# A decoder layer on one core: the causal mask of stick-breaking attention moves from TensorE to VectorE, and 1/rms per token comes back through DRAM

## The chip, the core and the metric

The kernel runs on one core of a Trainium2 chip. Five engines work side by side, each through its own instructions in order: TensorE (PE in the profile; its weight loads are PEld), VectorE (DVE), ScalarE (ACT), GpSimd (POOL) and SyncE (SP), which issues DMAs. Matrix products accumulate in PSUM, in banks of 128 partitions by 512 floats; everything else lies in SBUF, a 128-partition memory. Engines wait for each other on semaphores. The metric is the device time of one launch in microseconds (us).

## The reference, cut to what matters

One layer on 512 tokens of width 1024 (`D`): RMSNorm, one wide input projection, three attention branches (sliding window, stick-breaking, memory cross-attention), gates, an output projection, and a SwiGLU block. Two pieces matter here.

```
def rms_norm(x, g):
    y = xf * lax.rsqrt(jnp.mean(xf * xf, axis=-1, keepdims=True) + EPS)
    return y * g

def stick_breaking_attention(q, k, v):          # 8 heads of 64, blocks of 128 tokens
    z = einsum('bqhd,bkhd->bhqk', q_block, k[:, :L]) * d ** -0.5
    causal = arange(L)[None, :] < t
    log_1m = where(causal, log_sigmoid(-z), 0.0)
    between = cumsum(log_1m, axis=3, reverse=True) - log_1m
    a = where(causal, exp(log_sigmoid(z) + between), 0.0)
    out = einsum('bhqk,bkhd->bqhd', a, v)
```

## The kernel before, in words

Numbers are float32 throughout. A float32 matrix is cut into a high and a low part (`hi`, `lo`), and a product is three products of the fast 32-bit type (`mm3`, lines 164 to 168): ScalarE makes the high part (line 134), VectorE the low part (line 135). A plain float32 product, as in `mm` of line 171 with float32 operands, takes two passes on TensorE.

All weights pass through one stream, `dn`: a list of units, each of which has a load (SyncE), a split (ScalarE, VectorE) and a generator of products. The attention code of each head is a generator too; it gives up control with `yield us`, and `dn.run(us)` then emits so many microseconds of the stream's products by the kernel's own cost figures. These products are what TensorE has to do while the other engines work on the head. The framework's scheduler then fixes the order of every engine's instructions from priorities and its own estimates; on the chip each engine keeps to that order and waits where a semaphore is not there yet.

The normalization is applied late: projections run on x times the gain, and 1/rms multiplies their results. `rstd_of` (lines 218 to 234) takes per-position sums of squares `acc` (128 partitions; for the memory tokens two halves of 256 side by side). A product with an all-ones matrix adds over partitions and gives the sums on every partition, `ss`; four (two) products of one column give the same sums with a token per partition, `st`. Two reciprocal square roots follow: `rb`, token along the free axis, used where a projection is transposed; and `rs`, token on the partition, used where values are written (`v_all`, lines 333 to 339, and the memory values, line 398). The sum over the memory tokens, tile `mT`, is built by three GpSimd adds (line 368).

`sb_head` (lines 605 to 670) does one stick-breaking head. Keys lie on partitions, queries along the free axis, so the scores z are the upper part of a 4-by-4 grid of blocks: three PSUM banks hold 512, 384 and 256 + 128 columns (z of 0, 1 and 2; `SEG`). Eight score products fill them. Then four bf16 products of an identity with `negm` (-1e30 on and below the diagonal) are added onto the diagonal blocks: the mask (lines 626 and 627). For each bank ScalarE takes Abs, Exp and Ln, VectorE makes log(1 + e^z) from it (line 636, tile `e`), rounds it (`sh`, line 641) and takes the rest (`sl`, line 642). The head then yields 7.0 us. After that, products with triangular and all-ones matrices add the running sums onto the same three banks (lines 649 to 658, "the sums" below), ScalarE takes Exp, and two heads together are multiplied with the values into `ysb`, whose high part is `y10h` for the first pair.

PSUM has six banks for this work (`aps`), so two heads' scores fill them; the scores of head n+2 can only come when the banks of head n are free. Names with a number, as in the order below, are buffers of the program: a head's three banks are three numbers in a row. Projections that stand between the heads are `ka`, `qa`, `pmk` (memory keys), `pmv` and the gates `g`.

Of the kernel before, what the change touches and what calls it, by code (L numbers as in the profile page):

```python
# [10 lines left out]
F32 = mybir.dt.float32  # L11
F32R = mybir.dt.float32r
BF16 = mybir.dt.bfloat16
AF = mybir.ActivationFunctionType
ALU = mybir.AluOpType
AX = mybir.AxisListType

P = 128
D = 1024
S = 512  # L20
# [83 lines left out]
def tile_kernel(ctx, tc, a):  # L104
    nc = tc.nc
# [6 lines left out]
    drm = ctx.enter_context(tc.tile_pool(name="drm", bufs=1, space=bass.MemoryType.DRAM))  # L112
# [3 lines left out]
    cst = first.enter_context(tc.tile_pool(name="cst", bufs=1))  # L116

    def ck(name, dt=F32):
        return ckp.tile([P, 512], dt, tag="ck", name=name)

    def small(name, n=4):
        return sm.tile([P, 8], F32, tag="s", name=name)[:, :n]
# [4 lines left out]
    def aps(name):  # L127
        return psa.tile([P, 512], F32, tag="a", name=name)

    st = {}  # L130
# [33 lines left out]
    def mm3(out, l, r, start, stop):  # L164
        (lh, ll), (rh, rl) = l, r
        nc.tensor.matmul(out, lh, rh, start=start, stop=False, skip_group_check=True)  # L166
        nc.tensor.matmul(out, lh, rl, start=False, stop=False, skip_group_check=True)  # L167
        nc.tensor.matmul(out, ll, rh, start=False, stop=stop, skip_group_check=True)  # L168

    def mm(out, l, r, start, stop):  # L170
        nc.tensor.matmul(out, l, r, start=start, stop=stop, skip_group_check=True)  # L171

    def cols(hl, o, n):
        return hl[0][:, o : o + n], hl[1][:, o : o + n]
# [7 lines left out]
    def fn(*args, **kw):  # L182

        ins = nc.scalar.activation(*args, **kw)  # L184
        for p in pin:
            after(ins, p)
        since.append(ins)
        return ins
# [10 lines left out]
    def const(name, shape, pool=cst):  # L199
        t = pool.tile(shape, F32, name=f"c_{name}")  # L200
        nc.sync.dma_start(t[:, :], a[name])
        return t
# [3 lines left out]
    ones = cst.tile([P, P], F32, name="ones")  # L206
    nc.vector.memset(ones[:, :], 1.0)

    def rsqrt(r, v, t, ss):

        fn(t, ss, AF.Ln, bias=eps_t, scale=1.0 / D)
        nc.vector.tensor_scalar(v, ss, 1.0 / D, EPS, op0=ALU.mult, op1=ALU.add)
        fn(r, t, AF.Exp, scale=-0.5)
        nc.vector.scalar_tensor_tensor(t, r, -0.5, r, op0=ALU.mult, op1=ALU.mult)
        nc.vector.tensor_tensor(t, t, v, op=ALU.mult)
        nc.vector.scalar_tensor_tensor(r, t, 1.5, r, op0=ALU.add, op1=ALU.mult)

    def rstd_of(name, acc, n, bank):


        w = acc.shape[1] // n
        ps = bank(f"ss_{name}")
        for i in range(w):
            mm(ps[:, :n], ones[:, :], acc[:, i * n : (i + 1) * n], i == 0, i == w - 1)
        pt = bank(f"st_{name}")[:, : n // P] if n == S else ps[:, n : n + n // P]
        for t in range(n // P):
            for i in range(w):
                mm(pt[:, t : t + 1], acc[:, i * n + t * P : i * n + (t + 1) * P], ones[:, :1], i == 0, i == w - 1)
        rb = cst.tile([P, n], F32, name=f"rb_{name}")
        v, t = ck(f"v_{name}"), ck(f"t_{name}")  # L230
        rsqrt(rb[:, :], v[:, :n], t[:, :n], ps[:, :n])
        rs = cst.tile([P, n // P], F32, name=f"rs_{name}")
        rsqrt(rs[:, :], small(f"v_{name}", n // P), small(f"t_{name}", n // P), pt)
        return rs, rb

    def gained(x, g, h, l):
# [85 lines left out]
    def val(h, q):  # L322
        def gen(hi, lo):
            if q == 0:
                st["pv"] = [aps(f"pv{h}{t}") for t in range(NT)]
            for i in range(3 if q < 2 else 2):
                k = 3 * q + i
                for t in range(NT):
                    x = (u[k][0][:, t * P : (t + 1) * P], u[k][1][:, t * P : (t + 1) * P])
                    mm3(st["pv"][t][:, :320], x, cols((hi, lo), i * 320, 320), k == 0, k == KC - 1)  # L330
                    yield 0.41
                    if k == KC - 1:
                        nc.vector.tensor_scalar(
                            v_all[:, t * 640 + h * 320 : t * 640 + (h + 1) * 320],
                            st["pv"][t][:, :320],
                            st["rs"][:, t : t + 1],
                            None,
                            op0=ALU.mult,
                        )

        return gen

    v_all = cst.tile([P, NT * 640], F32, name="v_all")

    def vcols(t, lo):
        return v_all[:, t * 640 + lo : t * 640 + lo + 64]
# [87 lines left out]
    for h in range(2):  # L434
        for q in range(3):
            n = 3 if q < 2 else 2
# [111 lines left out]
    ident = const("ident", [P, P], base)  # L548
    ntri = const("ntri", [P, P])
    nmf = const("negm", [P, P])  # L550
    sinks = cst.tile([P, 8], F32, name="sinks")
    nc.sync.dma_start(sinks[:, :], a["sinks"].to_broadcast([P, 8]))
    identb = cst.tile([P, P], BF16, name="identb")
    nc.gpsimd.tensor_copy(identb[:, :], ident[:, :])
    negm = cst.tile([P, P], BF16, name="negmb")
    nc.gpsimd.tensor_copy(negm[:, :], nmf[:, :])
    ntri_r = cst.tile([P, P], F32R, name="ntri_r")
    nc.gpsimd.tensor_copy(ntri_r[:, :], ntri[:, :])
    none = cst.tile([P, P], F32, name="none")
# [38 lines left out]
    SEG = [(0, 0, 512), (1, 0, 384), (2, 0, 256), (2, 256, 128)]  # L598
    W = [512, 384, 384]

    def pair_out(b, c, ps):

        y[(b, c)] = parts(f"y{b}{c}", ps)

    def sb_head(h):
        c = h // 2
        ks, qs, ql = (st[(x, c, h % 2)] for x in ("kbs", "qbs", "qbl"))
        z = [aps(f"z{h}{i}") for i in range(3)]

        def seg(ts, j):  # L610
            i, o, n = SEG[j]
            return ts[i][:, o : o + n]

        for j in range(4):
            i, o, n = SEG[j]
            kj = slice(j * P, (j + 1) * P)
            if j < 3:
                out, qh, qlo = z[i][:, o : o + n], qs[:, j * P :], ql[:, j * P :]
            else:

                out = z[i][:, o : o + 2 * n]
                qh = qs[:, j * P :].unsqueeze(1).to_broadcast([P, 2, P])
                qlo = ql[:, j * P :].unsqueeze(1).to_broadcast([P, 2, P])
            mm(out, ks[:, kj], qh, j < 3, False)
            mm(out, ks[:, kj], qlo, False, False)
        for i, o, n in SEG:
            mm(z[i][:, o : o + P], identb[:, :], negm[:, :], False, False)
        e = [ck(f"e{h}{i}") for i in range(3)]
        sh = [ck(f"sh{h}{i}", F32R) for i in range(3)]
        sl = [ck(f"sl{h}{i}", F32R) for i in range(3)]  # L630
        for i in range(3):
            x, n = e[i][:, : W[i]], W[i]
            nc.scalar.activation(x, z[i][:, :n], AF.Abs)
            fn(x, x, AF.Exp, scale=-1.0)
            st["chain"] = fn(x, x, AF.Ln, bias=1.0)
            nc.vector.scalar_tensor_tensor(x, z[i][:, :n], 0.0, x, op0=ALU.max, op1=ALU.add)
            if i == 2:

                nc.vector.tensor_tensor(e[i][:, 384:], e[i][:, 128:256], e[i][:, 256:384], op=ALU.add)
                x, n = e[i][:, :], 512  # L640
            nc.vector.tensor_copy(sh[i][:, :n], x)
            nc.vector.tensor_tensor(sl[i][:, :n], x, sh[i][:, :n].bitcast(F32), op=ALU.subtract)
        yield 7.0

        def both(t):

            return t[2][:, :].rearrange("p (b n) -> p b n", b=4)[:, 0:4:3, :]

        for j in range(3):
            for t in (sh, sl):  # L650
                mm(seg(z, j), ntri_r[:, :], seg(t, j), False, j == 2 and t is sl)
        for t in (sh, sl):
            mm(z[0][:, 128:], none_r[:, :], seg(t, 1), False, False)
        for t in (sh, sl):
            mm(z[0][:, 256:], none_r[:, :], both(t), False, t is sl)
            mm(z[1][:, 128:384], none_r[:, :], both(t), False, t is sl)
        mm(z[2][:, 128:256], none[:, :], seg(e, 3), False, True)
        mm(seg(z, 3), ntri[:, :], seg(e, 3), False, True)
        for i in range(3):
            fn(e[i][:, : W[i]], z[i][:, : W[i]], AF.Exp)  # L660
        yield 3.0
        if h % 2 == 0:
            st["even"] = e
            return

        ys = aps(f"ysb{c}")
        for j in range(4):
            for i, x in enumerate((st["even"], e)):
                mm(ys[64 * i : 64 * i + 64, j * P :], vcols(j, 128 + (2 * c + i) * 64), seg(x, j), j == 0, j == 3)
        pair_out(SB, c, ys)  # L670
# [112 lines left out]
    for h in range(8):  # L783
        for us in sb_head(h):
            dn.run(us)
# [297 lines left out]
    rb = {}  # L1083
    bank = {}
# [316 lines left out]
```

## Time and profile before

| what | value |
|---|---|
| median of 3 runs | 818.17 us (818.04 to 818.42) |
| the profiled execution: its own time, and the span in the trace | 818.05 us, 816.3 us |
| TensorE busy | 806.5 us, 4753 products |
| VectorE busy | 590.2 us |
| ScalarE busy | 440.2 us |
| granted TensorE clock, mean | 0.999 |

A row of a timeline has the start in us from the span's beginning, the length in us, engine, line, operation, output and inputs, shapes, and how often it stands in a row (x). In brackets is how long the engine was idle before it and what ended that. An engine with Q behind its name (SPq) is the part that issues. A product's row on PE is longer than the time until the next one starts, since products overlap; what one costs in a row of others is the distance between two starts. The eight heads fill the stretch from 81 us to 215 us.

### The profile page before, as it was taken

How to read it: one execution, taken by the hardware profiler on the slowest of the kernel's cores; microseconds unless marked ns; L12 is line 12 of the kernel's file. 1: busy time of each engine (PE TensorE's matmuls, PEld its weight loads, DVE VectorE, ACT ScalarE, POOL GpSimd, SP SyncE). 2: the span in 40 equal slices, each digit the busy share in tenths (PEclk: the TensorE clock that was granted, in tenths of full speed). 3: DMA queues.
4: the chain of work that ended last, by engine and by line, in shares of the span. 5: the costliest groups of instructions: out<-in, count | busy, mean ns of one | idle time of the engine just before them, and what ended most of it. 6: DMA issues, size and time to landing. Idle time of an engine off the chain costs nothing.

```text
span 816.3 us, 12397 instructions
## 1 busy us (share of the span) xinstructions
PE 806.5 (99%) x4753; PEld 706.6 (87%) x4753; DVE 590.2 (72%) x945; ACT 440.2 (54%) x791; POOL 82.7 (10%) x100
## 2 busy tenths in 40 slices
PE   9999999999999999999999999999999999999996
PEld 6899888778788888888888899999999999988885
DVE  7796768556488853774385869977776767798797
ACT  7453757556555542553362666644444455666573
POOL 3002200000000000231003200010000000205200
PEclk9999999999999999999999999999999999999999
DMA  7434524321221223212359945977777763759902
GB/s 267 141 114 128 190 87 128 85 73 52 78 78 53 78 78 102 79 53 78 103 155 352 254 93 142 247 199 201 183 189 178 185 178 94 169 131 223 213 1 103
DMA packets 37563, 112.93 MB, mean 138 GB/s; under 512 B 4352, under 2 KB 6064, under 8 KB 37504
## 3 DMA queue, kind: packets, MB, share of 16 engines
q1 hardware_dynamic: 29184, 86.32, 33.5%
q0 software_dynamic: 7888, 25.43, 16.4%
q8 instruction: 37, 0.61, 0.3%
q10 hardware_dynamic: 432, 0.39, 0.1%
q14 instruction: 22, 0.18, 0.1%
HBM read 108.46 MB, written 3.67 MB: 137 GB/s over the span
## 4 chain that ended last, share of the span: by engine, by line
PE 94%; DVE 3%; ACT 1%; DMA 1%; issue 0%; ACTq 0%; SPq 0%; DVEq 0%
PE g L166 5%; PE g L167 5%; PE g L168 5%; PE gx L166 5%; PE gx L168 5%; PE gx L167 5%; PE z L171 4%; PE br L166 3%; PE br L167 3%; PE br L168 3%; PE gy L168 3%; PE gy L166 3%; PE gy L167 3%; PE x L167 2%; PE x L166 2%; PE x L168 2%
## 5 line engine op out<-in xcount | busy, mean ns | idle before, releaser
L134 ACT CAST hi<-raw 128x1024 fp32r<-128x1024 f32 (+2 forms) x64 | 65.8, 1034 | 110.1 <-issue 50.2
L134 ACT CAST hi<-gw 128x1024 fp32r<-128x1024 f32 x77 | 79.8, 1048 | 82.2 <-DVE gw L986 40.0
L135 DVE TENSOR_TENSOR lo<-gw,hi 128x1024 fp32r<-128x1024 f32 x77 | 93.5, 1223 | 33.6 <-ACT hi L134 33.6
L135 DVE TENSOR_TENSOR lo<-raw,hi 128x1024 fp32r<-128x1024 f32 (+2 forms) x64 | 78.1, 1220 | 17.6 <-ACT hi L134 17.3
L166 PE MATMUL g<-uh,hi 128*128 128x512 f32 x192 | 75.6, 394 | 0.0
L168 PE MATMUL g<-uh,lo 128*128 128x512 f32 x192 | 74.8, 389 | 0.0
L167 PE MATMUL g<-ul,hi 128*128 128x512 f32 x192 | 74.8, 389 | 0.0
L288 DVE SCALAR_TENSOR_TENSOR g<-g,rb_x 128x512 f32<-128x512 f32 x24 | 16.4, 690 | 55.4 <-PE g L168 55.3
L168 PEld LDWEIGHTS g<-uh,lo 128*128 128x128 f32 x192 | 36.0, 188 | 7.6
L166 PEld LDWEIGHTS g<-uh,hi 128*128 128x128 f32 x192 | 36.1, 188 | 7.5 <-issue 0.3
L968 POOL DMA_DIRECT2D gw<-in_w_gu x27 | 23.4, 905 | 188.8 <-DMA gw<-in_w_gu 81.4
L167 PEld LDWEIGHTS g<-ul,hi 128*128 128x128 f32 x192 | 36.1, 188 | 7.1
L134 ACT CAST hi<-r 128x1024 fp32r<-128x1024 f32 (+1 forms) x24 | 23.6, 982 | 19.9 <-PE y L168 5.3
L167 PE MATMUL x<-lo,lh 128*128 128x512 f32 x88 | 34.2, 389 | 0.0
L166 PE MATMUL x<-hi,lh 128*128 128x512 f32 x88 | 34.2, 389 | 0.0
L168 PE MATMUL x<-hi,ll 128*128 128x512 f32 x88 | 34.1, 389 | 0.0
L135 DVE TENSOR_TENSOR lo<-r,hi 128x1024 fp32r<-128x1024 f32 (+1 forms) x24 | 27.1, 1131 | 3.7 <-ACT hi L134 3.6
L184 ACT ACTIVATE e<-e 128x384 f32<-128x384 f32 (+1 forms) x48 | 26.9, 561 | 1.5
L134 ACT CAST hi<-bp 128x512 fp32r<-128x512 f32 x33 | 19.1, 619 | 13.4 <-PE y L168 4.8
L135 DVE TENSOR_TENSOR lo<-bp,hi 128x512 fp32r<-128x512 f32 x33 | 22.3, 711 | 5.0 <-ACT hi L134 4.9
L166 PE MATMUL gx<-T4h,hi 128*128 128x256 f32 x88 | 25.1, 285 | 0.4 <-ACT hi L134 0.4
L166 PE MATMUL gy<-N22h,hi 128*128 128x256 f32 x88 | 25.1, 285 | 0.2 <-ACT hi L134 0.2
(546 smaller groups left out, 2618.1 us busy)
## 6 DMA issues: line engine op xcount, KB each, us to landing
gw<-in_w_gu SPq DMA_DIRECT2D x57, 512.0 KB, 5.1
raw<-in_w_p SPq DMA_DIRECT2D x38, 512.0 KB, 3.6
gw<-in_w_gu POOLq DMA_DIRECT2D x27, 512.0 KB, 7.9
raw<-in_w_br SPq DMA_DIRECT2D x12, 512.0 KB, 3.8
bp<-in_w_dn SPq DMA_DIRECT2D x22, 256.0 KB, 8.4
r<-in_w_dn POOLq DMA_DIRECT2D x10, 512.0 KB, 8.7
raw<-in_w_out SPq DMA_DIRECT2D x8, 512.0 KB, 3.6
bp<-in_w_dn POOLq DMA_DIRECT2D x11, 256.0 KB, 12.8
```

The costliest lines, as they stand in the source:

```text
L134: ins = nc.scalar.copy(hi, raw)
L135: lows = nc.vector.tensor_tensor(lo, raw, hi.bitcast(F32), op=ALU.subtract)
L166: nc.tensor.matmul(out, lh, rh, start=start, stop=False, skip_group_check=True)
L167: nc.tensor.matmul(out, lh, rl, start=False, stop=False, skip_group_check=True)
L168: nc.tensor.matmul(out, ll, rh, start=False, stop=stop, skip_group_check=True)
L171: nc.tensor.matmul(out, l, r, start=start, stop=stop, skip_group_check=True)
L184: ins = nc.scalar.activation(*args, **kw)
L288: nc.vector.scalar_tensor_tensor(t[:, :], ps[:, :], s, st["rb"][:, :], op0=ALU.mult, op1=ALU.mult)
L968: nc.gpsimd.dma_start(gw[(n, key)][:, :], g_src(n, i, j), accum_op=ALU.add)
```

## The change: mask on VectorE, 1/rms per token by DMA

Three things change. First, the four mask products of each head go, and with them the bf16 copies of the identity and of `negm` that GpSimd made; instead VectorE adds the float32 `negm` onto the diagonal block of each bank in PSUM, one instruction for each of the first two banks (128 columns) and one for the two blocks of the third (2 x 128). The head's first yield is 8.5 instead of 7.0. Second, the one-column products and the second reciprocal square root go; the first row of `rb` is written to DRAM and read back with a token per partition, by two DMAs of GpSimd, the second waiting for the first. For the memory tokens the two halves of the sums of squares are now added by VectorE, so that one product of ones is left of two. Third, the evictions into `v_all` are emitted at high priority.

```
     def rstd_of(name, acc, n, bank):
-        w = acc.shape[1] // n
+        if acc.shape[1] > n:
+            nc.vector.tensor_tensor(acc[:, :n], acc[:, :n], acc[:, n : 2 * n], op=ALU.add)
         ps = bank(f"ss_{name}")
-        for i in range(w):
-            mm(ps[:, :n], ones[:, :], acc[:, i * n : (i + 1) * n], i == 0, i == w - 1)
-        pt = bank(f"st_{name}")[:, : n // P] if n == S else ps[:, n : n + n // P]
-        for t in range(n // P):
-            for i in range(w):
-                mm(pt[:, t : t + 1], acc[:, i * n + t * P : i * n + (t + 1) * P], ones[:, :1], i == 0, i == w - 1)
+        mm(ps[:, :n], ones[:, :], acc[:, :n], True, True)
         rb = cst.tile([P, n], F32, name=f"rb_{name}")
         v, t = ck(f"v_{name}"), ck(f"t_{name}")
         rsqrt(rb[:, :], v[:, :n], t[:, :n], ps[:, :n])
+        row = drm.tile([1, n], F32, name=f"row_{name}")
+        nc.gpsimd.dma_start(row[:, :], rb[:1, :])
         rs = cst.tile([P, n // P], F32, name=f"rs_{name}")
-        rsqrt(rs[:, :], small(f"v_{name}", n // P), small(f"t_{name}", n // P), pt)
+        nc.gpsimd.dma_start(rs[:, :], row[:, :].rearrange("o (t p) -> (o p) t", p=P))
         return rs, rb
...
                     if k == KC - 1:
-                        nc.vector.tensor_scalar(
+                        with tc.high_priority():
+                            nc.vector.tensor_scalar(
...
     def sb_head(h):
...
-        for i, o, n in SEG:
-            mm(z[i][:, o : o + P], identb[:, :], negm[:, :], False, False)
+        for i in range(3):
+            x, m = z[i][:, :P], nmf[:, :]
+            if i == 2:
+                x, m = z[i][:, :].rearrange("p (b n) -> p b n", b=4)[:, 0:4:2, :], m.unsqueeze(1).to_broadcast([P, 2, P])
+            nc.vector.tensor_tensor(x, x, m, op=ALU.add)
...
-        yield 7.0
+        yield 8.5
```

The order of the built program moves with it. Lines of the changed file are a few lower than those before.

**First place: VectorE at the first two heads.** Before, after the last instruction that belongs to the bias (`brow`), VectorE goes straight to head 0, whose banks are z_887, z_888 and z_889:

```order
L582 TENSOR_TENSOR brow<-pbias,wm 128x384
L636 SCALAR_TENSOR_TENSOR e_902<-z_887,e_902 128x512
L641 CAST sh_905<-e_902 128x512
L642 TENSOR_TENSOR sl_908<-e_902,sh_905 128x512
L636 SCALAR_TENSOR_TENSOR e_903<-z_888,e_903 128x384
L641 CAST sh_906<-e_903 128x384
L642 TENSOR_TENSOR sl_909<-e_903,sh_906 128x384
```

In the changed program the banks of head 0 are z_873 to z_875 and those of head 1 z_1045 to z_1047:

```order
L578 TENSOR_TENSOR brow<-pbias,wm 128x384
L627 TENSOR_TENSOR z_873<-z_873,c_negm 128x128
L627 TENSOR_TENSOR z_874<-z_874,c_negm 128x128
L627 TENSOR_TENSOR z_875<-z_875,c_negm 128x2x128
L627 TENSOR_TENSOR z_1045<-z_1045,c_negm 128x128
L627 TENSOR_TENSOR z_1046<-z_1046,c_negm 128x128
L627 TENSOR_TENSOR z_1047<-z_1047,c_negm 128x2x128
L636 SCALAR_TENSOR_TENSOR e_887<-z_873,e_887 128x512
L641 CAST sh_890<-e_887 128x512
L642 TENSOR_TENSOR sl_893<-e_887,sh_890 128x512
L636 SCALAR_TENSOR_TENSOR e_888<-z_874,e_888 128x384
L641 CAST sh_891<-e_888 128x384
```

The masks of head 0 come first, as written. Then the three masks of head 1 stand ahead of everything that VectorE does for head 0 after its mask (`e_887` and on). On TensorE the scores of head 1 come behind the 24 products of `ka`, and directly behind them the sums of head 0. This is TensorE in the changed program from the last score product of head 1 on:

```order
L171 MATMUL z_1047<-qbl_428,kbs_305 128x256
L171 MATMUL z_1047<-qbs_427,kbs_305 128x256
L171 MATMUL z_1047<-qbl_428,kbs_305 128x256
L171 MATMUL z_873<-sh_890,ntri_r 128x512
L171 MATMUL z_873<-sl_893,ntri_r 128x512
L171 MATMUL z_874<-sh_891,ntri_r 128x384
L171 MATMUL z_873<-sh_891,none_r 128x384
L171 MATMUL z_874<-sl_894,ntri_r 128x384
L171 MATMUL z_873<-sl_894,none_r 128x384
L171 MATMUL z_875<-sh_892,ntri_r 128x256
L171 MATMUL z_873<-sh_892,none_r 128x256
L171 MATMUL z_874<-sh_892,none_r 128x256
```

Between the scores of head 1 and the sums of head 0 nothing else stands, neither before nor now; before, the four masks stood there.

**Second place: TensorE at heads 2 and 3.** Before, the products with the values of the first pair (`ysb`) were followed by all eight scores of head 2 and its masks, and 54 products of `pmk` later by the sums of head 2. In the changed program the four score products of head 2's first two banks went ahead, and the third bank's scores follow the values:

```order
L171 MATMUL ysb_1228<-e_1061,v_all 64x128
L171 MATMUL z_1243<-qbs_466,kbs_309 128x256
L171 MATMUL z_1243<-qbl_467,kbs_309 128x256
L171 MATMUL z_1243<-qbs_466,kbs_309 128x256
L171 MATMUL z_1243<-qbl_467,kbs_309 128x256
L166 MATMUL pmk_1206<-mh_811,hi_1034 128x256
L167 MATMUL pmk_1206<-ml_812,hi_1034 128x256
```

From here 27 products of `pmk` with 256 columns follow, the first two of which end the rows above; then the scores of head 3 (z_1408 to z_1410) and the sums of head 2 (z_1241 to z_1243) alternate:

```order
L171 MATMUL z_1408<-qbs_472,kbs_312 128x512
L171 MATMUL z_1408<-qbl_473,kbs_312 128x512
L171 MATMUL z_1241<-sh_1258,ntri_r 128x512
L171 MATMUL z_1409<-qbs_472,kbs_312 128x384
L171 MATMUL z_1409<-qbl_473,kbs_312 128x384
L171 MATMUL z_1241<-sl_1261,ntri_r 128x512
L171 MATMUL z_1410<-qbs_472,kbs_312 128x256
L171 MATMUL z_1410<-qbl_473,kbs_312 128x256
L171 MATMUL z_1410<-qbs_472,kbs_312 128x256
L171 MATMUL z_1410<-qbl_473,kbs_312 128x256
L171 MATMUL z_1242<-sh_1259,ntri_r 128x384
L171 MATMUL z_1241<-sh_1259,none_r 128x384
```

Eight more products on the second and the third bank follow, the last three of them with `sl_1263`, and one with an `e` ends the sums. On VectorE the three masks of head 3 stand inside head 2's work: one of z_1408 and one of z_1409 ahead of `e_1256`, one of z_1410 ahead of `sh_1259`. What moved: `pmk` products that stood between the values and head 2's sums now stand ahead of the values.

**Third place: VectorE at heads 4 and 5.** Before, the third bank of head 4:

```order
L636 SCALAR_TENSOR_TENSOR e_1567<-z_1552,e_1567 128x384
L639 TENSOR_TENSOR e_1567<-e_1567 128x128
L641 CAST sh_1570<-e_1567 128x512
L135 TENSOR_TENSOR lo_1610<-raw_1495,hi_1609 128x1024
L642 TENSOR_TENSOR sl_1573<-e_1567,sh_1570 128x512
```

In the changed program the first mask of head 5 (z_1711) stands in the middle of it:

```order
L636 SCALAR_TENSOR_TENSOR e_1581<-z_1567,e_1581 128x384
L639 TENSOR_TENSOR e_1581<-e_1581 128x128
L627 TENSOR_TENSOR z_1711<-z_1711,c_negm 128x128
L641 CAST sh_1584<-e_1581 128x512
L135 TENSOR_TENSOR lo_1621<-raw_1507,hi_1620 128x1024
L642 TENSOR_TENSOR sl_1587<-e_1581,sh_1584 128x512
```

On TensorE the eight scores of head 5 stand, now as before, among the sums of head 4, ahead of the products with head 4's last `sl`.

More of the change, by code (lines that the diff above doesn't have):

```diff
@@ L332, in gen @@
                     if k == KC - 1:
[L333 to L339, printed above, removed]
+                        with tc.high_priority():
+                            nc.vector.tensor_scalar(
+                                v_all[:, t * 640 + h * 320 : t * 640 + (h + 1) * 320],
+                                st["pv"][t][:, :320],
+                                st["rs"][:, t : t + 1],
+                                None,
+                                op0=ALU.mult,
+                            )
         return gen
@@ L552, in tile_kernel @@
     nc.sync.dma_start(sinks[:, :], a["sinks"].to_broadcast([P, 8]))
[L553 to L556, printed above, removed]
     ntri_r = cst.tile([P, P], F32R, name="ntri_r")
```

## The prediction

> **What bounds the kernel now.** I read the page's busy times first, then the chain that ended last, then windows over the stretches in which the heads run.
>
> ```profile
> PE 806.5 (99%) x4753; PEld 706.6 (87%) x4753; DVE 590.2 (72%) x945; ACT 440.2 (54%) x791; POOL 82.7 (10%) x100
> PE 94%; DVE 3%; ACT 1%; DMA 1%; issue 0%; ACTq 0%; SPq 0%; DVEq 0%
> 80.00:88.50 8.50, 8.50 (x48) 6.89 (x47) 5.19 (x12) 5.09 (x10) 1.07 (x1) 1.00 0.71 246
> 88.50:95.00 6.50, 6.38 (x39) 5.48 (x38) 4.50 (x11) 3.40 (x7) 3.92 (x6) 1.00 0.53 155
> 114.00:128.00 14.00, 14.00 (x106) 12.60 (x105) 9.46 (x16) 8.67 (x14) 0.00 (x0) 1.00 0.21 53
> 157.00:163.00 6.00, 6.00 (x39) 5.43 (x38) 5.14 (x8) 2.50 (x4) 0.00 (x0) 1.00 0.40 99
> ```
>
> In a window the figures after its length are the busy times of PE, PEld, DVE, ACT and POOL, then the granted clock. TensorE sets the time: it is busy in 806.5 of 816.3 us and in nearly all of the four stretches. So a product that goes is time gained, and any wait that TensorE has not now is time lost. VectorE has idle time (72% busy), but it works in order, and what it makes TensorE wait for is the question of this case.
>
> **What is removed.** The mask of head 0, the one-column products of x, and both sums of the memory tokens, on TensorE:
>
> ```profile
> 82.96 0.40 PE L171 MATMUL z<-negmb,identb 128*128 128x128 bf16 x4
> 83.16 0.48 PE L166 MATMUL ka<-uh,hi 128*128 128x512 f32 x1
> 83.48 0.40 PE L167 MATMUL ka<-ul,hi 128*128 128x512 f32 x1
> 83.71 0.40 PE L168 MATMUL ka<-uh,lo 128*128 128x512 f32 x1
> 23.73 0.95 PE L171 MATMUL st_x<-ones,xacc 128*128 128x1 f32 x8
> 24.54 0.48 PE L166 MATMUL kb<-uh,hi 128*128 128x512 f32 x1
> 85.33 1.02 PE L171 MATMUL ss_m<-mT,ones 128*128 128x256 f32 x4
> 86.20 0.95 PE L171 MATMUL ss_m<-ones,mT 128*128 128x1 f32 x8
> 87.01 0.48 PE L166 MATMUL ka<-uh,hi 128*128 128x512 f32 x1
> ```
>
> The four mask products go from 82.96 to 83.16: 0.20 us. The product behind them needs 0.32 us to its successor (83.16 to 83.48), where the next needs 0.23 (83.48 to 83.71); those 0.09 us I count to the mask too. So 0.29 a head, 2.3 us for eight; 1.6 if the change of type costs the same elsewhere. The one-column products of x take 24.54 - 23.73 = 0.81. Of the memory tokens' sums half of 86.20 - 85.33 goes, 0.43, and the one-column products, 87.01 - 86.20 = 0.81. **Removed: 2.3 + 0.81 + 1.24 = 4.4 us**, at least 3.7.
>
> **What the masks cost on VectorE.** No row of before has VectorE writing PSUM, so the price is bounded by rows of the same operation or with one operand in PSUM:
>
> ```profile
> 81.67 0.56 DVE L582 TENSOR_TENSOR brow<-pbias,wm 128x384 f32<-128x384 f32 x1 [0.22 <-PE pbias L171]
> 85.18 0.69 DVE L636 SCALAR_TENSOR_TENSOR e<-z,e 128x512 f32<-128x512 f32 x1 [2.96 <-ACT e L184]
> 85.91 0.43 DVE L641 CAST sh<-e 128x512 fp32r<-128x512 f32 x1
> 88.43 0.55 DVE L636 SCALAR_TENSOR_TENSOR e<-z,e 128x384 f32<-128x384 f32 x1
> 89.02 0.29 DVE L639 TENSOR_TENSOR e<-e 128x128 f32<-128x128 f32 x1
> 89.76 1.22 DVE L135 TENSOR_TENSOR lo<-raw,hi 128x1024 fp32r<-128x1024 f32 x1
> 90.89 0.69 DVE L642 TENSOR_TENSOR sl<-e,sh 128x512 fp32r<-128x512 f32 x1
> ```
>
> 512 columns with z take 0.69 and 384 take 0.55, so 128 columns are 0.14 and the fixed part about 0.13: 0.27 for 128 columns, 0.41 for two blocks of 128. The 128-column row of line 639 (0.29) agrees. Bounds: 0.15 (the slope alone) and 0.69 (the longest row with z) for each. A head's three masks are 0.95, eight heads 7.6 us of VectorE; alone these lie beside TensorE. What matters is where they stand.
>
> **First stall: heads 0 and 1.** By the order shown ahead, head 1's masks stand in VectorE's queue before the first instruction that head 0 needs from it (`e_887`). They need head 1's scores. On TensorE these come after the 24 products of `ka`, and directly behind them come head 0's sums, which need `sh` and `sl`. So the chain of VectorE for head 0, which ran beside `ka` from 85.18 to 91.58 (90.89 + 0.69), now begins only when head 1's last score has landed, and TensorE has nothing else in its queue.
>
> ```profile
> 91.66 0.28 PE L171 MATMUL z<-qbl,kbs 128*128 128x256 f32 x1
> 91.78 0.40 PE L171 MATMUL z<-negmb,identb 128*128 128x128 bf16 x4
> 91.99 0.48 PE L171 MATMUL z<-sh,ntri_r 128*128 128x512 f32 x1
> 93.58 0.28 PE L171 MATMUL z<-sl,ntri_r 128*128 128x256 f32 x1
> ```
>
> From the issue of the last score (the row at 91.66) to the third bank's `sl`: the score's own length 0.28, the third mask 0.41 (the first two end earlier), the chain 91.58 - 85.18 = 6.40, a handover 0.05: 7.14 us. In that time TensorE does the score's own 0.12 (91.66 to 91.78) and the sums that do not need the last `sl`, 1.5 (91.99 to 93.58 is 1.59; a little of it comes late). **Stall 7.14 - 1.62 = 5.5 us.** With masks at 0.15 it is 5.2, at 0.69 5.8; if the `lo` of 1.22, which stands in the chain in both programs, finds another place, 4.4.
>
> **Second stall: heads 2 and 3.** Now 54 products of `pmk` stand between head 2's masks and its sums; in the changed program 27, and the third bank's scores come only behind the values. ScalarE, in order, makes `y10h` before it starts on head 2:
>
> ```profile
> 116.52 0.59 ACT L134 CAST y10h<-ysb 128x512 fp32r<-128x512 f32 x1 [3.18 <-PE ysb L171]
> 118.08 0.60 ACT L633 ACTIVATE e<-z 128x512 f32<-128x512 f32 x1 [0.98 <-PE z L171]
> 125.69 0.68 DVE L642 TENSOR_TENSOR sl<-e,sh 128x512 fp32r<-128x512 f32 x1
> ```
>
> From `y10h` to the last `sl` of head 2 it is 126.37 - 116.52 = 9.85; the idle 0.98 for z disappears, since its first banks stand ready, so 8.87. Head 3's three masks stand inside this chain, 0.95, and the wait between queues another 0.15: 9.95. TensorE's work from the last value product to the products with that last `sl`, at the distances of before (0.12 for 256 columns, 0.17 for 384, 0.23 for 512): the four scores 0.5, 27 `pmk` products 3.2, head 3's scores (0.46 + 0.35 + 0.46 = 1.3), and those sums of head 2 that stand ahead, some 1.5. Together 6.5. **Stall 9.95 - 6.5 = 3.4 us**; without the masks' share 2.5, with masks at 0.69 4.5.
>
> **Third stall: heads 4 and 5.** The first mask of head 5 stands before the rounding of head 4's third bank (`sh_1584`), and waits for head 5's first scores, which TensorE emits in the middle of head 4's sums.
>
> ```profile
> 157.71 0.43 DVE L641 CAST sh<-e 128x512 fp32r<-128x512 f32 x1
> 159.19 0.69 DVE L642 TENSOR_TENSOR sl<-e,sh 128x512 fp32r<-128x512 f32 x1
> ```
>
> From that score's issue: 0.23 to the second of the two, its length 0.39, mask 0.27, then `sh` to the end of `sl`, 159.88 - 157.71 = 2.17, handover 0.1: 3.16. TensorE has 1.64 of head 5's remaining scores and head 4's sums to do meanwhile. **Stall 1.5 us** (1.4 to 2.0 with the mask's bounds). Between head 6's last score and its sums the changed order has 39 products of 512 columns, 9.0 us at 0.23; the chain there, as at head 2 from ScalarE's first row for z, is 126.37 - 118.08 = 8.3, and the sums with the last `sl` come later still. So nothing there, and the same for head 7.
>
> Strict order within VectorE's queue carries all three. [...] No single row of before decides it outright.
>
> **What I cost at nothing.** The round trip of 1/rms: `rb_x` is ready at 28.5, and the first reader of `rs_x` is `v_all` at 66.7.
>
> ```profile
> 27.79 0.69 DVE L216 SCALAR_TENSOR_TENSOR rb_x<-t_x,rb_x 128x512 f32<-128x512 f32 x1
> bscr<-brow POOLq DMA_DIRECT2D x1, 1536.0 KB, 6.5
> bias<-bscr POOLq DMA_DIRECT2D x4, 256.0 KB, 6.0
> 15.69 4.45 POOL L268 MEMSET qbl<- 64x512 f32 x8
> 66.71 1.92 DVE L333 TENSOR_SCALAR v_all<-pv,rs_x 128x320 f32<-128x320 f32 x4
> 66.86 1.28 POOL L368 TENSOR_TENSOR mT<-mT,mT 128x512 f32<-128x512 f32 x1 [1.09 <-ACT mT L364]
> 67.30 0.42 PE L166 MATMUL pv<-hi,uh 128*128 128x320 f32 x1 [0.33 <-DVE v_all L333]
> ```
>
> The nearest DMAs of GpSimd (a write to DRAM, 6.5 us, and reads of it, 6.0) make 13 us: landed at about 42, cover 25 us. The eight memsets of `qbl`, 4.45 us, stand behind the two DMAs on GpSimd now; they would end before 50, and head 0 needs them at 81. If the cover were gone, `v_all` and with it TensorE would wait for the rest.
>
> The halves of the memory sum are a case of their own: VectorE adds them ahead of a `lo` and of `v_all`, and must wait for GpSimd's third add, which ends at 68.14 (66.86 + 1.28). If that stays, the first `v_all` ends at 68.14 + 0.42 + 0.81 + 0.48 and TensorE goes on at 69.9 instead of 67.30: +2.6. GpSimd's adds start when the memory tiles have come, and these loads stand behind a weight load whose buffer is freed by a VectorE instruction that the new order puts some 2 us earlier, TensorE being 0.8 ahead as well. I take 0; bounds -0.3 (the wait of 0.33 that `v_all` causes now) and +2.6.
>
> **The sum.** -4.4 + 5.5 + 3.4 + 1.5 = +6.0. On the profiled execution's 818.05 (span 816.3, and 1.75 around it, which the change leaves) that is 824.05; the median is 0.1 above the profiled execution. Forecast **824.0**. Its own bounds: -4.4 + 4.4 + 2.5 + 1.4 = +3.9 and -3.7 + 5.8 + 4.5 + 2.0 = +8.6, so 821.9 to 826.7.
>
> **The rivals.**
> - *Only the first pair stalls* (0.10). The first stall has nothing in TensorE's queue to cover it; the other two are differences of two estimated sums of 10 and 3 us. If the masks are half as long and the stream's products suffice there: -4.4 + 5.5 = +1.1, 819.2. Against it: half of `pmk` has left the place.
> - *The memory sum holds `v_all` up* (0.10): 6.0 + 2.6 = +8.6, 826.6. For it the rows at 66.71 and 66.86: GpSimd's add ends after `v_all` starts. Against it the earlier loads.
> - *The other side: the order does not hold TensorE up* (0.05). VectorE takes a mask when its scores are there and does head 0's work before; then only the removal stays, -4.4, 813.7. It decides if less than 4.4 of stalls is left. For it: VectorE has 28% idle. Against it: each row of VectorE in the first chain starts where the one before ends, in the order written.
> - *The clock falls in the gaps* (0.06).
>
> ```profile
> 810.00:814.00 4.00, 0.00 (x0) 0.00 (x0) 2.55 (x6) 0.71 (x4) 0.00 (x0) 1.00 0.50 187
> 814.00:816.30 2.30, 0.00 (x0) 0.00 (x0) 0.00 (x0) 0.00 (x0) 0.00 (x0) 0.60 0.25 93
> ```
>
> At the end TensorE does nothing from 810 on; the clock is 1.00 for four more us and 0.60 after them. The forecast's longest single gap is about 2 us (mask, `e`, `sh` of the first bank), with sums in between, so I expect 1.00. If half speed came for 4 us of one stall, 2 us more: 826 for one, 830 for all three. [...]
> - *`rs_x` late* (0.03): if the round trip took 50 us instead of 13, `v_all` would wait until 78, up to 11 us more, 835.
>
> **How the numbers follow.** Forecast 0.66, rivals 0.10, 0.10, 0.05, 0.06, 0.03. No change means within 0.2%, 1.6 us, which is what a measurement of this kernel can tell. Slower by more: forecast, memory sum, clock and late `rs_x`, 0.85, less 0.01 for the forecast's lower end, 0.84; within: the first-pair case, 0.09, and that 0.01, 0.10; faster: 0.05 and 0.01 of the first-pair case with less stall, 0.06. The range takes in the first-pair case below and the memory sum above: **819.0 to 827.0**; out stay the faster side, the clock, late `rs_x` and a little of each edge.
>
> **What would show it.** Right: VectorE idle for about 6 us between head 0's masks and its first `e`, ended by TensorE's scores of head 1; TensorE with some 5.5, 3.4 and 1.5 us of idle, ended by VectorE, at the three places; the masks' rows at 0.27 and 0.41; `v_all` started by products, not by GpSimd; the two small DMAs landed long before 60. Wrong: TensorE full at these places, or a wait of TensorE elsewhere, above all at 67 or in front of heads 6 and 7.

## The result and the profile after

The changed kernel takes 826.83 us (826.54 to 827.39), the kernel before beside it 818.31 us (818.04 to 818.81). The ratio is 1.0105, 95% interval 1.009 to 1.012: 8.5 us slower. The forecast was 824.0 with a range of 819.0 to 827.0. The sign, the three places and their sizes came as forecast. Two terms did not: less work was left than I had counted, and the TensorE clock fell to half after two of the stalls, a case that I had given 0.06.

The page of the changed kernel, TensorE's and the chain's line:

```profile
PE 807.7 (98%) x4703; PEld 705.0 (85%) x4703; DVE 595.0 (72%) x962; ACT 440.0 (53%) x787; POOL 83.9 (10%) x102
PE 91%; DVE 4%; issue 1%; DMA 1%; ACT 1%; POOL 0%; ACTq 0%; DVEq 0%; SPq 0%; POOLq 0%
```

Fifty products fewer, and yet TensorE is busy for longer: 807.7 against 806.5 us. That points to slower products, though products that stand apart also count for longer, since their rows no longer overlap (a row of 256 columns has 0.28 us, and among others the next starts after 0.12); the windows below decide it. The view of what TensorE waited for (in us, number of times, the longest) gives the places; before, of these three rows only the last was there, with 0.3:

```profile
PE z L171 <- DVE sh L641: 3.9, 5, 1.6
PE z L171 <- DVE sl L642: 3.2, 4, 1.1
PE pv L166 <- DVE v_all L333: 0.9, 1, 0.9
```

These waits count only from the modelled end of the product before; what a stall costs is read from the distance of starts. VectorE of the changed kernel at the first two heads:

```profile
82.96 0.43 DVE L627 TENSOR_TENSOR z<-z,c_negm 128x256 f32<-128x256 f32 x1 [0.18 <-PE z L171]
89.35 0.65 DVE L627 TENSOR_TENSOR z<-z,c_negm 128x128 f32<-128x128 f32 x2 [5.96 <-PE z L171]
90.18 0.43 DVE L627 TENSOR_TENSOR z<-z,c_negm 128x256 f32<-128x256 f32 x1 [0.18 <-PE z L171]
90.52 0.68 DVE L636 SCALAR_TENSOR_TENSOR e<-z,e 128x512 f32<-128x512 f32 x1
96.24 0.68 DVE L642 TENSOR_TENSOR sl<-e,sh 128x512 fp32r<-128x512 f32 x1
```

VectorE idles for 5.96 us in front of head 1's masks, with head 0's work behind them in its queue, until TensorE has done head 1's scores. Then the whole chain runs, from 90.52 to 96.92, and TensorE has to wait for its pieces:

```profile
89.86 0.28 PE L171 MATMUL z<-qbl,kbs 128*128 128x256 f32 x1
91.71 0.49 PE L171 MATMUL z<-sh,ntri_r 128*128 128x512 f32 x1 [1.57 <-DVE sh L641]
96.98 0.58 PE L171 MATMUL z<-sl,ntri_r 128*128 128x256 f32 x1 [0.73 <-DVE sl L642]
97.79 0.63 PE L171 MATMUL z<-e,none 128*128 128x128 f32 x2
98.07 0.77 PE L166 MATMUL qa<-uh,hi 128*128 128x512 f32 x1
101.38 0.39 PE L168 MATMUL qa<-uh,lo 128*128 128x512 f32 x1
```

From the last score of head 1 to the last row of head 0's sums (`e,none`) it takes 97.79 - 89.86 = 7.93 us. In the eight `qa` products after it nothing waits any more, and still they take 101.38 - 98.07 = 3.31 us, 0.41 each instead of 0.23. The windows tell why (columns as in the prediction; the last figures are granted clock, DMA share and GB/s):

```profile
90.00:94.25 4.25, 1.98 (x7) 0.93 (x6) 3.93 (x8) 0.51 (x2) 3.03 (x5) 1.00 0.74 238
94.25:101.00 6.75, 5.58 (x17) 4.19 (x17) 6.37 (x13) 2.09 (x4) 0.37 (x1) 0.50 0.26 86
101.25:104.00 2.75, 2.75 (x15) 2.31 (x14) 1.48 (x2) 0.00 (x0) 0.74 (x1) 1.00 0.09 9
131.00:135.00 4.00, 2.23 (x11) 1.20 (x9) 3.90 (x9) 2.07 (x3) 0.00 (x0) 1.00 0.00 0
135.25:138.50 3.25, 2.74 (x9) 2.45 (x10) 2.95 (x5) 1.91 (x4) 0.00 (x0) 0.50 0.57 164
175.30:177.00 1.70, 0.59 (x4) 0.38 (x4) 1.70 (x3) 0.00 (x0) 0.00 (x0) 1.00 0.00 0
```

From 94.25 to 101 and from 135.25 to 138.5 TensorE runs at half speed (granted clock 0.50). It had not been idle for long at a time: the longest wait ahead of the first was 1.57 us, and TensorE was busy for 1.98 of the 4.25 us before the clock fell.

The second and third stall, TensorE's rows and the row of VectorE that holds the third up:

```profile
131.12 0.28 PE L171 MATMUL z<-qbl,kbs 128*128 128x256 f32 x1
135.76 0.58 PE L171 MATMUL z<-sl,ntri_r 128*128 128x256 f32 x1 [1.12 <-DVE sl L642]
174.42 0.30 DVE L627 TENSOR_TENSOR z<-z,c_negm 128x128 f32<-128x128 f32 x1 [2.04 <-PE z L171]
176.83 0.39 PE L171 MATMUL z<-sl,ntri_r 128*128 128x256 f32 x1 [1.11 <-DVE sl L642]
```

And the 1/rms part, by GpSimd's DMAs (with the landing time of the second), the addition of the two halves, and `v_all`:

```profile
28.90 0.68 POOL L230 DMA_DIRECT2D row_x<-rb_x  x1 [13.30 <-DVE rb_x L216]
32.13 0.82 POOL L232 DMA_DIRECT2D rs_x<-row_x  x1 [2.55 <-DMA row_x<-rb_x]
rs_x<-row_x POOLq DMA_DIRECT2D x1, 2.0 KB, 4.0
65.39 0.47 DVE L222 TENSOR_TENSOR mT<-mT 128x256 f32<-128x256 f32 x1 [2.73 <-POOL mT L368]
66.52 1.91 DVE L333 TENSOR_SCALAR v_all<-pv,rs_x 128x320 f32<-128x320 f32 x4
67.11 0.41 PE L166 MATMUL pv<-hi,uh 128*128 128x320 f32 x1 [0.91 <-DVE v_all L333]
```

`rs_x` is there at 36, thirty us ahead of its reader. But VectorE waits 2.73 us for GpSimd in front of the addition, and `v_all` stands behind it.

### The profile page after: what moved, and what is told of

Same layout as the page of the kernel before. It is cut to its first block, busy times and chain, and to the rows that moved or that the text cites. A ratio compares the mean times of both kernels' runs of the same rounds, so it can differ in the third digit from the quotient of the medians.

```text
span 825.0 us, 12304 instructions
## 1 busy us (share of the span) xinstructions
PE 807.7 (98%) x4703; PEld 705.0 (85%) x4703; DVE 595.0 (72%) x962; ACT 440.0 (53%) x787; POOL 83.9 (10%) x102
## 4 chain that ended last, share of the span: by engine, by line
PE 91%; DVE 4%; issue 1%; DMA 1%; ACT 1%; POOL 0%; ACTq 0%; DVEq 0%; SPq 0%; POOLq 0%
PE g L166 5%; PE g L167 5%; PE g L168 5%; PE gx L166 5%; PE gx L168 5%; PE gx L167 5%; PE z L171 3%; PE br L166 3%; PE br L167 3%; PE br L168 3%; PE gy L168 3%; PE gy L166 3%; PE gy L167 3%; PE x L168 2%; PE x L167 2%; PE x L166 2%
## 5 line engine op out<-in xcount | busy, mean ns | idle before, releaser
L184 ACT ACTIVATE e<-z 128x384 f32<-128x384 f32 (+1 forms) x24 | 11.6, 527 | 32.5 <-PE z L171 28.7
```

## The experiments

All medians in us; "before" is the kernel before beside the same runs.

| kernel | median | before | ratio (95% interval) |
|---|---|---|---|
| the change | 826.83 | 818.31 | 1.0105 (1.009 to 1.012) |
| masks behind the chain | 816.19 | 818.19 | 0.9978 (0.9969 to 0.9988) |
| the change, no masks | 814.13 | 818.19 | 0.9953 (0.9937 to 0.997) |
| the change with fillers | 824.58 | 818.19 | 1.0078 (1.0063 to 1.0093) |
| 1/rms alone | 815.67 | 818.19 | 0.9972 (0.9961 to 0.9982) |
| the change, yield 7.0 | 821.28 | 818.26 | 1.0036 (1.0023 to 1.0048) |
| masks behind, yield 7.0, halves on GpSimd | 811.44 | 818.26 | 0.9915 (0.9901 to 0.9928) |
| the same, yield 9.5 | 812.42 | 818.26 | 0.9927 (0.9915 to 0.994) |
| 1/rms alone, halves on GpSimd | 814.70 | 818.26 | 0.9953 (0.9941 to 0.9966) |
| masks behind, yield 7.0, halves on GpSimd; no masks | 811.75 | 818.00 | 0.9922 (0.9908 to 0.9936) |
| before, no masks | 814.41 | 818.00 | 0.9958 (0.9944 to 0.9972) |

**The masks' place.** `after` is the kernel's own helper: it orders two instructions of one engine.

```
+            masked = nc.vector.tensor_tensor(x, x, m, op=ALU.add)
+            if "last" in st:
+                after(masked, st["last"])
...
+            last = nc.vector.tensor_tensor(sl[i][:, :n], x, sh[i][:, :n].bitcast(F32), op=ALU.subtract)
+        st["last"] = last
         yield 8.5
```

> The changed kernel with one edit: each mask of a head stands on VectorE behind the last `sl` of the head before it; the same instructions in all, TensorE's order unchanged but for ten rows around head 4. Theory (the masks' place in VectorE's queue makes the stalls): heads 0 and 1 lose the whole stall and its slow clock, 7.4 us, heads 4 and 5 lose 1.4, and of heads 2 and 3 the masks' 0.95 goes while the moved `pmk` products still leave some 2.5 us: 816 to 817 us, clock 1.00 at heads 0 and 1. Rival (the masks cost by what they are: writes into the banks that TensorE uses, 7.6 us of VectorE): little changes, 823 or more.

Measured: 816.19, 10.6 us below the change with the same instructions. VectorE and TensorE of this kernel at the first two heads:

```profile
83.86 0.69 DVE L638 SCALAR_TENSOR_TENSOR e<-z,e 128x512 f32<-128x512 f32 x1 [1.03 <-ACT e L184]
96.21 0.82 DVE L627 TENSOR_TENSOR z<-z,c_negm 128x128 f32<-128x128 f32 x3
```

```profile
89.29 0.28 PE L171 MATMUL z<-qbl,kbs 128*128 128x256 f32 x1
90.92 0.28 PE L171 MATMUL z<-sl,ntri_r 128*128 128x256 f32 x1
91.27 0.38 PE L171 MATMUL z<-e,none 128*128 128x128 f32 x2
91.41 0.48 PE L166 MATMUL qa<-uh,hi 128*128 128x512 f32 x1
93.34 0.39 PE L168 MATMUL qa<-uh,lo 128*128 128x512 f32 x1
126.57 0.38 PE L171 MATMUL z<-sl,ntri_r 128*128 128x256 f32 x1 [1.12 <-DVE sl L644]
```

Head 0's chain begins at 83.86 instead of 90.52, beside `ka`, and head 1's masks come at 96.2. From the last score to `e,none` it is 1.98 us instead of 7.93, and the eight `qa` products take 1.93 instead of 3.31. So the first stall cost 5.95 + 0.14 (from `e,none` to `qa`) + 1.38 = 7.5 us. Of this the slow clock has the 1.38, the 0.14 and, in the sums behind the last wait, (97.79 - 96.98) - (91.27 - 90.92) = 0.46: 2.0 us. The wait itself is 5.5. At heads 2 and 3 a stall is left (the row at 126.57 ends it), as expected, since the `pmk` products have moved: by the distances of starts about 2.3 us, counted as for the second stall further down. So most of the second stall belongs to the moved products, and only the rest to the masks. The times of this kernel go from 815.0 to 817.4, wider than the others'. The trace is of one of the shorter (815.59); what made the others longer is not shown.

**No masks.** The loop that adds the masks is left out of the changed kernel.

> The changed kernel without the masks: the 24 additions are left out, so z is not masked; nothing is put in their place, and all engines keep the order of the changed kernel otherwise (16 rows of TensorE differ). Theory (place, not price): 0.3 to 1 us below the kernel with the masks behind the chain, 815 to 816.5 us, since 24 instructions in their right place lie beside TensorE's work. Rival (price): 3 us or more below that kernel.

Measured: 814.13, 2.1 below the masks-behind kernel, between the two expectations; the two profiled executions (815.59 and 814.33) are 1.3 apart. In their traces that comes from order, not from a price of the additions. The masks-behind kernel has a wait of 0.6 us at 142 (0.8 by the starts) that this one has not, and its last pair's value products stand in two groups instead of one, which costs 1.0 us (shown with the last experiment of this part); against that, `v_all` holds TensorE up for 0.3 us longer here: 1.5 together. The pair at the end asks again without waits around.

**Fillers.**

```
+        def fill(n):
+            for _ in range(n if h in (0, 2) else 0):
+                mm(z[0][:, :], idle[:, :P], idle[:, :], False, False)
...
+            fill(n)     # 3 behind the first sl, 4 behind the second, 5 behind the third sh
```

> The changed kernel with more work for TensorE: at heads 0 and 2 twelve products of zeros each (512 columns, 0.22 us each, 5.3 us together) are added onto the head's first bank inside its waits: three behind the first `sl`, four behind the second, five behind the third `sh`. The result stays the same. Theory (half clock after a stretch with many short gaps costs 1.9 us at heads 0 and 1 and 1.2 at heads 2 and 3): the clock stays at 1.00 and the kernel comes out faster with more work, 823.5 to 824.5 us. Rival (only a long single gap lowers the clock, or the slow products were waiting for something else): 826.8 us or more.

Measured: 824.58, just above the expected stretch: by the ratios 2.2 us faster than the change, with 24 products more. Its windows:

```profile
90.00:93.00 3.00, 1.56 (x5) 0.77 (x7) 2.86 (x7) 0.00 (x0) 2.45 (x5) 1.00 0.89 276
93.25:96.25 3.00, 3.00 (x10) 1.62 (x9) 2.93 (x6) 0.00 (x0) 0.00 (x0) 0.50 0.10 41
96.50:104.00 7.50, 7.50 (x39) 5.95 (x38) 5.31 (x10) 2.65 (x6) 1.27 (x2) 1.00 0.25 72
123.00:135.00 12.00, 11.45 (x72) 8.36 (x70) 8.38 (x18) 7.09 (x12) 0.00 (x0) 1.00 0.11 40
```

At heads 2 and 3 the clock stays at 1.00, with TensorE busy for 11.45 of 12.00 us. At heads 0 and 1 it still falls to 0.50, behind the first wait of 1.6 us, which has no fillers in it, but it is back at 96.5 instead of 101, while VectorE's chain is still running. The mean granted clock of all four executions, 0.996 to 0.998 against 0.990 to 0.992 in the change, says the same. So where the gaps between products were filled, at heads 2 and 3, the clock did not fall, and the slow clock is a cost of its own: the kernel with more work is 2.2 us faster, and it still has one slow stretch.

**1/rms alone.** `rstd_of` and the `v_all` lines of the change, all else as before.

> The kernel before with the 1/rms half of the change alone (DRAM round trip, no one-column products, high priority of `v_all`); masks stay on TensorE. Theory: 0.81 and 1.24 us of products go, the wait at the first `v_all` grows by 0.58: 818.3 - 1.5 = 816.8 us. Rival (the round trip or GpSimd's DMAs cost something later): 818.3 us or more.

Measured: 815.67, 1.1 better than expected. The sums' places show 2.2 us less (the stretch from `ss_x` to the second `kb` product behind it falls from 24.85 - 22.87 = 1.98 to 1.09, that of `ss_m` from 87.33 - 85.33 = 2.00 to 0.67), and a wait at `v_all` of 1.1 instead of 0.3. Of the rest, 0.45 us of the profiled execution lies ahead of `ss_x` (22.42 instead of 22.87), behind the same 83 products; the start of `ss_x` goes from 22.37 to 23.23 in the traces of these kernels, so I do not count that to this edit. What is left I could not place. Then the addition of the halves on GpSimd:

```
-            nc.vector.tensor_tensor(acc[:, :n], acc[:, :n], acc[:, n : 2 * n], op=ALU.add)
+            nc.gpsimd.tensor_tensor(acc[:, :n], acc[:, :n], acc[:, n : 2 * n], op=ALU.add)
```

> The kernel with the 1/rms half of the change alone, with the two halves of the memory sum added by GpSimd instead of VectorE. Theory (VectorE's addition waits for GpSimd and holds up `v_all` behind it): the wait of TensorE at the first `v_all` falls from 1.1 to some 0.3 us, 815.7 - 0.8 = 814.9 us. Rival (`v_all` is late for another reason): 815.7 us as before.

Measured: 814.70, as expected. The row that waited, with VectorE's addition, and VectorE at the same place without it:

```profile
64.97 0.47 DVE L222 TENSOR_TENSOR mT<-mT 128x256 f32<-128x256 f32 x1 [2.72 <-POOL mT L368]
```

```profile
64.12 1.92 DVE L333 TENSOR_SCALAR v_all<-pv,rs_x 128x320 f32<-128x320 f32 x4
```

`v_all` now starts at 64.1, and TensorE does not wait there at all. The addition's wait for GpSimd was the cause.

**The yield.** `yield 8.5` back to `yield 7.0`, nothing else.

> The changed kernel with the head's first yield at 7.0 as before, the masks where the scheduler puts them. In the order head 1's masks still stand ahead of head 0's chain on VectorE, with head 0's sums right behind head 1's scores; but 6 us of products instead of 3.6 stand in front of head 2's sums, and no mask stands inside the chains of heads 2 and 4. Theory (each stall follows from place and cover): the first stall and its slow clock stay (7.4 us), the second and third go (4.6 + 1.4 us): 826.8 - 6.0 = 820 to 821.5 us. Rival (8.5 has nothing to do with it): 826 us or more.

Measured: 821.28, within the theory's bounds. The second and third stall are gone, the first stands. Its windows:

```profile
90.00:92.50 2.50, 0.69 (x3) 0.28 (x2) 2.29 (x5) 0.47 (x2) 2.46 (x4) 1.00 0.78 220
92.75:102.75 10.00, 8.81 (x25) 6.71 (x25) 9.47 (x18) 3.39 (x7) 1.17 (x3) 0.50 0.32 99
```

The waits stand at the same five products as in the change, but here the clock fell at 92.5 and stayed low until 102.8.

**All three mended.** Masks behind the chain, halves on GpSimd, and the yield at 7.0 or at 9.5.

> The changed kernel with three edits: the masks behind the last `sl` of the head before, the yield at 7.0, and the addition of the memory sum's two halves on GpSimd, which made the sums, instead of VectorE. Theory: no wait of TensorE at the heads, and the wait at the first `v_all` back from 0.9 to 0.3 us, since VectorE no longer waits for GpSimd ahead of it: 812.5 to 814 us, faster than the masks-behind kernel by 2 to 3. Rival (something else holds the masks-behind kernel back): 815.5 us or more.

> As the kernel before this one in the call, with the yield at 9.5: by the order every head has 6.2 us or more of products between its last score and its sums. Theory: the same, 812.5 to 814 us; the size of the yield matters only by the cover that it happens to leave. Rival: a larger yield is worse by itself, 815 us or more.

Measured: 811.44 and 812.42, both below what was expected, the first by 1.1. Both are well below the kernel before; the first, 0.9915 of it, by 6.8 us. The two are 1.0 apart where the same was expected; neither has a wait of TensorE at the heads or at `v_all`, and the cause of the 1.0 is open. The TensorE line of the first and two windows:

```profile
PE 800.9 (99%) x4703; PEld 702.6 (87%) x4703; DVE 594.0 (73%) x961; ACT 440.0 (54%) x787; POOL 86.5 (11%) x103
```

```profile
80.00:88.00 8.00, 8.00 (x38) 6.41 (x37) 6.14 (x14) 5.93 (x11) 0.90 (x1) 1.00 0.68 254
88.00:98.00 10.00, 10.00 (x54) 8.68 (x53) 8.38 (x16) 5.93 (x12) 5.02 (x8) 1.00 0.60 176
```

The same 4703 products as in the change take 6.8 us less of TensorE.

**The price of a mask, on either engine.** The masks left out of the kernel just shown, and out of the kernel before.

> The kernel with masks behind, yield 7.0 and the halves on GpSimd, without the masks: the 24 additions are left out, z is not masked. Theory (in their place, with enough products for cover, the masks' 7.6 us of VectorE lie beside TensorE and cost nothing): 811.0 to 811.8 us, the same as with them. Rival (they still cost a part, by delaying the heads or VectorE's other work): 810.5 us or less.

> The kernel before without its masks: the 32 bf16 products of the identity with the masking matrix are left out, z is not masked. By the price of the prediction, 0.29 us a head, 2.3 us go: 815.9 us. By the two kernels without any wait (1/rms alone with the halves on GpSimd, 814.70, and the same with the masks on VectorE, 811.44) the masks on TensorE are worth up to 3.3 us: 814.9 us.

Measured: 811.75 without the masks on VectorE, against 811.44 with them: no cost that these runs can tell, since the intervals of the ratios lie on each other. And 814.41 without the masks on TensorE, 3.6 us less than before, where eight times 0.29 is 2.3. At the masks' own places the trace of before has no more than the 0.29. Of the other 1.3 us, 1.0 is a matter of order. Before, the first two rows of the last pair's value products stand alone among head 7's sums, and fourteen follow; in the kernel without masks (last row) all sixteen stand together:

```profile
208.27 1.07 PE L171 MATMUL ysb<-e,v_all 128*64 128x512 f32 x2
213.00 2.37 PE L171 MATMUL ysb<-e,v_all 128*64 128x512 f32 x14
209.17 2.38 PE L171 MATMUL ysb<-e,v_all 128*64 128x512 f32 x16
```

By the next row's start the two take 1.00 us (to 209.27), the fourteen 2.29 (to 215.29), and the sixteen together 2.31 (to 211.48). Before, all four pairs stand in two groups; in the change and in the kernel of 811.44 one pair stands together. The other 0.3 is not placed.

## Why the prediction was right, and where it was not

| step | predicted | what the runs showed |
|---|---|---|
| removed work | -4.4 | -6.8: the kernel of 811.44, the change with all three mends, no waits |
| first stall | +5.5 | +5.5, and 2.0 of slow clock behind it |
| second stall | +3.4 | about +3.3, and 1.3 of slow clock |
| third stall | +1.5 | about +1.3 |
| memory sum ahead of `v_all` | 0 | +0.9 against no wait |
| clock | 1.00 | 0.50 for 6.8 and 3.4 us |
| sum | +6.0 | +8.5; the rows above give 7.5, 1.0 is not placed |

The second stall's size is the excess of the distances between the products' starts, from 128 to 138 us, over the usual distances (the median of the same pair of shapes), less the same excess before: 4.6 us in all. Of these the five `pmv` products behind it have 0.8 and the last sums 0.5 at half speed. The third is the excess at the one gap (the row at 176.83). In the two profiled executions themselves, of the change and of the kernel of 811.44, less is open: their spans, 825.0 and 810.3 us, are 14.7 apart, and the rows from the first stall to `v_all` give 14.3.

**Luck in the sum.** 826.83 lies 0.17 us below the upper end of the range, and the range was drawn to leave the clock's case out. That case came, with 3.3 us, and `v_all` with 0.9; both had been put at nothing, and 2.4 us more of removed work took most of it back. The sign, the places and the waits were reasoned; that the time stayed inside the range is in part luck.

**Right: the order decides.** The masks of the next head stood in VectorE's queue ahead of the chain that TensorE needed next, and VectorE stood idle for 5.96 us with that chain behind them. That it does not pass a mask that waits was my assumption in the forecast; this idle time shows it. One edit of their place alone took 10.6 us away. It did not take all: most of the second stall comes from the products that moved ahead of the values, and it went, like the third, with the yield of 7.0. All three places were in the order before the run, and the wait was worked out from rows: a chain of 6.40 in the forecast, 90.52 to 96.92 in the trace. The masks themselves were put at 0.27 and 0.41; a lone 128-column mask takes 0.30 (the row at 174.42), one of two blocks 0.43. In a better place they cost nothing that the runs can tell (811.44 with them, 811.75 without).

**Right: the round trip is hidden.** Estimated 13 us, measured 7.2 from the first issue to the second landing (28.90 to 32.13 + 4.0).

**Mis-sized: the removed work.** I took only what the rows at the masks and the sums themselves show. The masks were worth 3.6 instead of 2.3, and 1/rms 3.6 instead of 2.05 (of this 0.3 is the wait at `v_all` that went). A price read at one place misses what the change of order does at the others: 1.0 us of the masks' part is the value products of one pair, which now stand together. About 1 us of 1/rms stays open.

**Failed: "The forecast's longest single gap is about 2 us ..., so I expect 1.00."** The gaps were as forecast (1.57 at most), and the clock still fell. The step took the longest gap as the measure. In the trace each fall came behind several shorter ones close together: 1.98 of 4.25 us busy with no wait over 1.57 at heads 0 and 1, 2.23 of 4.00 with none over 1.12 at heads 2 and 3. The price that I gave it, 2 us for one stall, was near the truth (2.0 and 1.3).

**Half right: the memory sum.** I had named the wait (bounds -0.3 and +2.6) and taken 0, since the tiles' loads would come earlier. They did: GpSimd's sums ended at about 65.4 instead of 68.1. But VectorE was earlier too, and waited for 2.73 us; the first `v_all` held TensorE up by 0.6 us more than before.

**The rivals.** That only the first pair stalls is what the yield of 7.0 gives, not the change. That VectorE's order does not hold TensorE up fell with the first row of 5.96 us. The memory sum gave 826.6 for another reason than the one that brought the time there: the measured 826.8 is the forecast with the clock's case added and the removed work larger.

## What to carry to other kernels

When work moves to an engine with free time, look first at which waiting instruction now stands ahead of what the bound engine needs next: here a new place for the same 24 additions took 10.6 us away, and with enough products for cover the kernel was no slower with them than without (811.44 and 811.75). Emit such work behind the chain of the stage before, and then see that each stage still has enough products between what it gives and what it needs back. Where several short waits of TensorE lie close together, check whether the granted clock falls behind them, and if it does, add the slow products to their price: here 2.0 us at heads 0 and 1 and 1.3 at heads 2 and 3.

## What the runs showed of the hardware

Read from windows of a quarter of a us (half a us with the fillers), the granted clock was 0.50 from 94.25 to 101.1 (6.8 us) and from 135.2 to 138.6 (3.4) in the change, from 93.1 to 96.5 (3.4) with the fillers, and from 92.5 to 102.8 (10.2) with the yield of 7.0. The place of the waits does not give the length: waits at the same five products of heads 0 and 1 were followed by 6.8 us of half speed in the change and by 10.2 with the yield of 7.0.

Nor does the busy share of a short stretch give the fall. Ahead of the two falls of the change TensorE was busy for 1.98 of 4.25 us and for 2.23 of 4.00, ahead of the one with the fillers for 1.56 of 3.00, and with the yield of 7.0 for 0.69 of 2.50. At the third stall of the change it was busy for 0.59 of 1.70 us, and there the clock stayed at 1.00. What sets the fall and the length no run shows.
